# Clipped differences of the scan's sums on GpSimd, and 4 KB runs of the sums in DRAM

## The chip, the cores and the metric

The kernel runs on one core of one Trainium2 chip. The metric is the device time of one execution in microseconds. PE is TensorE, DVE is VectorE, ACT is ScalarE, POOL is GpSimd, SP is the engine that issues most transfers.

## The reference

Two layers of a streaming encoder for 256 prompt frames and 64 sample frames (320 columns in all). The first layer is a Mamba-2 mixer and a convolutional feed-forward network, the second a latent attention and another feed-forward network. The change lies in the mixer's scan. Its 32 heads are in four groups of eight, and time is cut into chunks. Within a chunk, with `acs` the running sum of `dt * a` of a head,

```python
seg = acs[:, :, :, None] - acs[:, :, None]
decay = jnp.exp(jnp.where(causal, seg, -jnp.inf))
wts = cb[..., None] * decay * dtc[:, :, None]
y_diag = jnp.einsum('bclsge,bcsgep->bclgep', wts, xc)
```

so each head needs a square of decays, the Exp of the difference of two sums, `acs` at the later frame minus `acs` at the earlier one. All differences that count are at most zero; where the later frame is the earlier one in the square, the entry is masked.

## The kernel before

Everything is transposed: features on the 128 partitions, frames in the free dimension. Weights are streamed once from DRAM by SP (`wr`, three buffers), split into a high and a low part by ACT (`wh`, L326) and DVE (`wl`, L328), four buffers of each, and used by PE in three matmuls each (L283, L284); a `block` is 24 such matmuls for one 128x320 result. PE has far more of this work than of any other.

The scan takes its frames in three chunks, two of 128 frames (prompt) and one of 64 (sample). `ssm_dt` forms `acs`, 96 rows (three chunks of 32 heads) by 128 frames; `ssm_dt2` (L837) writes it to DRAM as `acd` (L841) and transposes it on PE to `dtt` (L850), which so holds a column for each head and chunk. For each group and chunk `ssd_fetch` (L852) reads eight rows of `acd` back, to all 128 partitions at once: `dc`, 128 x 8 x n (L861). For the second and third chunk four rows each go to the two halves of `ea` (L866). Then, head by head (L874), ACT forms

`Relu(-dc + dtt column)`, the earlier sum less the later one, not below zero,

and `ssd_decay` (L878) takes Exp of its negative, one chunk at a time (through the helper `exp`, L673). DVE multiplies by the masked products of B and C (`bcs`, L909), and PE takes the products with `xa`, the inputs times `dt` (L932), and with the state (L940).

`ssd_steps` gives the order of one group's steps for its chunks: `pre` (L903 to L909), `xpose` (transposes L915 and the two DVE products L922 that give `xa` and `xw`), `diag` (L932; for the first chunk ACT empties the result to `yg`, L934; for the others L940 to L943), `states` (L949 and on). All of them take PSUM from a pool of two buffers (`px`).

Around it, `PLAN` (L28) is an order written out by hand: blocks of projections (`conv`, `z`) with `fetch`, `decay`, `scan`, `silu` and `gate` between. `work(n)` after each block emits n of the scan's late steps and, at a pace set by `fetch`, the heads' steps of L874. The Tile framework then orders each engine's instructions by a simulated timeline with costs of its own, within the dependences; `after` adds dependences without a wait, such as those of `exp` and `silu` (L667 to L675), which keep ACT's Exps and Silus together, since going from one to the other loads a table. Transfers of `acd` are held behind the current block (`issue`, L658).

POOL, before, does the small copies of the convolutions in this stage: the pads of `ext` (L636, L637), which ACT's L647 reads, and the rows saved for the state (L643, L644). Elsewhere it does some adds and, in the attention, weight splits.

Of the kernel before, what the change touches and what calls it, by code (L numbers as in the profile page):

```python
# [11 lines left out]
AF = mybir.ActivationFunctionType  # L12
ALU = mybir.AluOpType
# [3 lines left out]
P = 128  # L17
# [68 lines left out]
class Kern:  # L86
# [590 lines left out]
    def ssm(self):  # L677
        nc, a = self.nc, self.a
        self.silus, self.exps, self.burst = [], [], []
        self.yg, self.dc, self.ea = {}, {}, {}  # L680
        with ExitStack() as st:
            dr = st.enter_context(self.tc.tile_pool(name="acd", bufs=1, space=bass.MemoryType.DRAM))
            self.acd = self.t(dr, [96, P], "acd")
            ap = self.pool(st, "ssma")
            ah = self.t(ap, [P, 16, T], "ah", F32R)
            al = self.t(ap, [P, 16, T], "al", F32R)
            with ExitStack() as s2:
# [4 lines left out]
                with ExitStack() as s3:  # L692
# [3 lines left out]
                    for k in range(KD):  # L696
                        r = self.raw[k] = self.t(dp, [P, 512], "w0", bufs=KD)
# [76 lines left out]
            for half in range(2):  # L774
                w = [self.nextw(), self.nextw()]
                for n in range(4):
# [3 lines left out]
                    p = ps[3] if m == 7 else self.px()  # L780
                    for kb in range(12, 16):
# [4 lines left out]
                        q = slice((kb % 2 * 4 + n) * 128, (kb % 2 * 4 + n) * 128 + 128)  # L786
# [50 lines left out]
    def ssm_dt2(self, dt2, sp, dp):  # L837
        nc = self.nc
        dt, acs, w = dt2

        self.issue(nc.sync.dma_start(out=self.acd, in_=acs))  # L841
        self.cd = self.t(sp, [P, 3, 32], "cd")
        for p, n in ((slice(0, 64), 128), (slice(64, 96), 64)):
            self.exp(w[p, 0:n], acs[p, 0:n], scale=-1.0, bias=acs[p, n - 1:n])
        nc.vector.tensor_tensor(out=w, in0=w, in1=dt, op=ALU.mult)
        pd = self.px()
        for i, t_ in enumerate((dt, w, acs)):
            nc.tensor.transpose(pd[:, 96 * i:96 * i + 96], t_, self.ident[0:96, 0:96])
        self.dtt = self.t(sp, [P, 288], "dtt")
        nc.vector.tensor_copy(out=self.dtt, in_=pd[:, 0:288])  # L850

    def ssd_fetch(self, g, sp):  # L852

        nc = self.nc
        self.dc[g], self.ea[g] = {}, {}

        def load():
            for c, (_, n) in enumerate(CHUNKS):
                r0 = 32 * c + 8 * g
                dc = self.dc[g][c] = self.t(sp, [P, 8, n], f"dc{c}", bufs=DCB)  # L860
                self.issue(nc.sync.dma_start(out=dc, in_=self.acd[r0:r0 + 8, 0:n].partition_broadcast(P)))  # L861
                if c > 0:
                    ea = self.ea[g][c] = self.t(sp, [P, 4, n], f"ea{c}", bufs=DCB)
                    for odd in range(2):
                        r = r0 + 4 * odd
                        self.issue(nc.sync.dma_start(out=ea[64 * odd:64 * odd + 64], in_=self.acd[r:r + 4, 0:n].partition_broadcast(64)))  # L866

        def head(c, h):
            n = CHUNKS[c][1]
            dc = self.dc[g][c]  # L870
            q = 32 * c + 8 * g + h
            if c and h == 0:
                nc.vector.tensor_copy(out=self.cd[:, c, 8 * g:8 * g + 8].unsqueeze(2), in_=dc[:, :, n - 1:n])
            nc.scalar.activation(out=dc[:n, h, :], in_=dc[:n, h, :], func=AF.Relu, scale=-1.0, bias=self.dtt[:n, 192 + q:193 + q])  # L874

        return load, [lambda c=c, h=h: head(c, h) for c in range(3) for h in range(8)]

    def ssd_decay(self, g):  # L878

        cd = self.cd[:, 1:3, 8 * g:8 * g + 8]  # L880
        self.exp(cd, cd)
        for c, (_, n) in enumerate(CHUNKS):
            dc = self.dc[g][c]
            self.exp(dc[:n], dc[:n], scale=-1.0)
            if c > 0:
                self.exp(self.ea[g][c], self.ea[g][c])

# [624 lines left out]
```

## Time and profile before

| what | value |
|---|---|
| median of 3 runs | 1002.08 us (999.59 to 1002.16) |
| profiled execution, its own time | 1002.07 us |
| its span | 1000.3 us |
| granted clock, mean | 0.983 |
| PE busy | 960.9 us |
| DVE busy | 746.7 us |
| ACT busy | 620.4 us |
| POOL busy | 337.1 us |

The span runs from the first to the last recorded instruction; the time has some 1.8 us more around it. Busy times are of the whole span and hide stages in which another engine is the limit. In rows of the timeline the first number is the start in us, the second the duration in us of the x instructions on that row together, and the brackets give the engine's idle time before it and what ended that. In rows of groups the numbers after the bar are busy us and mean ns of one.

### The profile page before, as it was taken

Reading aid. Unit: us, or ns where it says so; the run is one execution under the profiler, and the core shown is the slowest. Engines: PE = TensorE matmul, PEld = TensorE weight load, DVE = VectorE, ACT = ScalarE, POOL = GpSimd, SP = SyncE. Lnnn points to the kernel's source line nnn. Section 1 sums busy time; section 2 is a strip of 40 time slices with the busy share of each in tenths; the row PEclk is TensorE's granted clock in tenths of the full one; section 3 lists DMA queues with packets and bytes.
Section 4 is the critical chain, followed back from the end, with each engine's and each line's share of the span. In section 5 each row is a group of like instructions: output and inputs, shape, how many; then the busy total and the mean of one; then the engine's idle time right before and its main releaser. Section 6 shows DMA issues by size and latency. Waiting matters only on the chain.

```text
span 1000.3 us, 18088 instructions
## 1 busy us (share of the span) xinstructions
PE 960.9 (96%) x6585; PEld 930.1 (93%) x6585; DVE 746.7 (75%) x1425; ACT 620.4 (62%) x1285; POOL 337.1 (34%) x597
## 2 busy tenths in 40 slices
PE   8897999999999999999999999999999999999995
PEld 7897999979989999999998899999999999999994
DVE  7865888887677998784538898886538999775433
ACT  6589797833555687664544677775544778664330
POOL 3921321100044775430005765530004766441001
PEclk9998999999999999999999999999999999999998
DMA  7374637353324444455641222233443455444531
GB/s 262 108 213 143 211 125 224 115 172 90 117 74 141 156 150 158 156 157 178 194 139 35 86 67 69 56 106 98 148 145 96 136 170 168 149 144 143 151 116 53
DMA packets 50905, 135.54 MB, mean 136 GB/s; under 512 B 11488, under 2 KB 15232, under 8 KB 50816
## 3 DMA queue, kind: packets, MB, share of 16 engines
q1 hardware_dynamic: 50528, 134.06, 42.6%
q8 instruction: 51, 0.84, 0.4%
q14 instruction: 38, 0.31, 0.1%
q10 hardware_dynamic: 288, 0.33, 0.1%
HBM read 130.25 MB, written 4.12 MB: 134 GB/s over the span
## 4 chain that ended last, share of the span: by engine, by line
PE 80%; DVE 9%; ACT 5%; POOL 3%; issue 2%; DMA 1%; SPq 0%; POOLq 0%; ACTq 0%; DVEq 0%
PE pm L283 46%; PE pm L284 23%; PE px L283 2%; PE px L932 1%; ACT wh L326 1%; PE px L949 1%; PE px L284 1%; POOL xacc L442 1%; PE pr L362 1%; PE px L940 1%; ACT dc L874 1%; DVE wl L328 1%; POOL xn L478 1%; DVE y L450 1%; DVE x L454 1%
## 5 line engine op out<-in xcount | busy, mean ns | idle before, releaser
L326 ACT ACTIVATE wh<-wr 128x1024 fp32r<-128x1024 f32 (+4 forms) x235 | 228.0, 973 | 160.0 <-PE pm L283 141.9
L328 DVE TENSOR_TENSOR wl<-wr,wh 128x1024 fp32r<-128x1024 f32 (+2 forms) x204 | 244.2, 1197 | 110.4 <-ACT wh L326 109.3
L283 PE MATMUL pm<-xnh,wh 128*128 128x320 f32 x784 | 243.4, 312 | 3.9 <-ACT xnh L329 3.2
L283 PE MATMUL pm<-xnl,wh 128*128 128x320 f32 x784 | 244.6, 312 | 0.3 <-DVE xnl L330 0.3
L284 PE MATMUL pm<-xnh,wl 128*128 128x320 f32 x784 | 243.4, 311 | 0.0
L283 PEld LDWEIGHTS pm<-xnh,wh 128*128 128x128 f32 x784 | 147.5, 189 | 6.5 <-ACT xnh L329 3.8
L284 PEld LDWEIGHTS pm<-xnh,wl 128*128 128x128 f32 x784 | 147.8, 189 | 1.7 <-issue 1.7
L283 PEld LDWEIGHTS pm<-xnl,wh 128*128 128x128 f32 x784 | 147.9, 189 | 1.3 <-issue 0.7
L283 PE MATMUL pm<-ah,wh 128*128 128x320 f32 x452 | 139.8, 311 | 1.7 <-ACT ah L329 1.7
L284 PE MATMUL pm<-ah,wl 128*128 128x320 f32 x452 | 140.6, 311 | 0.0
L283 PE MATMUL pm<-al,wh 128*128 128x320 f32 x452 | 140.4, 311 | 0.0
L649 DVE SCALAR_TENSOR_TENSOR cv<-ext,vec,cv 128x322 f32<-128x322 f32 x176 | 96.7, 563 | 5.4 <-ACT cv L647 3.0
L636 POOL MEMSET ext<- 128x2 f32 (+1 forms) x112 | 10.8, 98 | 245.9 <-DVE al L330 83.2
L643 POOL COPY fsave<-ext 128x2 f32<-128x2 f32 x88 | 72.5, 823 | 53.6 <-ACT ext L640 49.3
L283 PEld LDWEIGHTS pm<-ah,wh 128*128 128x128 f32 x452 | 84.7, 188 | 2.5 <-ACT ah L329 2.0
L283 PEld LDWEIGHTS pm<-al,wh 128*128 128x128 f32 x452 | 85.1, 188 | 1.0 <-issue 1.0
L284 PEld LDWEIGHTS pm<-ah,wl 128*128 128x128 f32 x452 | 85.1, 188 | 1.0 <-issue 1.0
L328 POOL TENSOR_TENSOR wl<-wr,wh 128x512 fp32r<-128x512 f32 (+2 forms) x31 | 43.6, 1424 | 102.3 <-ACT wh L326 100.9
L283 PE MATMUL pm<-xgl,wh 128*128 128x320 f32 x220 | 68.3, 314 | 1.0 <-DVE xgl L426 1.0
L284 PE MATMUL pm<-xgh,wl 128*128 128x320 f32 x220 | 68.2, 313 | 0.7 <-DVE wl L330 0.7
L283 PE MATMUL pm<-xgh,wh 128*128 128x320 f32 x220 | 62.5, 316 | 2.8 <-ACT wh L329 1.3
L647 ACT ACTIVATE cv<-ext,vec 128x322 f32<-128x322 f32 x88 | 57.1, 654 | 9.5 <-POOL ext L637 6.6
(395 smaller groups left out, 2132.4 us busy)
## 6 DMA issues: line engine op xcount, KB each, us to landing
wr<-w_up SPq DMA_DIRECT2D x76, 512.0 KB, 3.3
wr<-w_in SPq DMA_DIRECT2D x37, 512.0 KB, 3.7
wr<-w_dn SPq DMA_DIRECT2D x32, 512.0 KB, 3.6
wr<-w_out SPq DMA_DIRECT2D x16, 512.0 KB, 3.4
wr<-w_o SPq DMA_DIRECT2D x16, 512.0 KB, 3.4
wr<-w_up_k SPq DMA_DIRECT2D x16, 384.0 KB, 3.2
wr<-w_dn SPq DMA_DIRECT2D x16, 384.0 KB, 3.2
dc<-acd SPq DMA_DIRECT2D x8, 512.0 KB, 6.4
```

The lines of the kernel that those rows point to most:

```text
L283: for i in (mm(out, wh, xh, start=first, stop=False), mm(out, wh, xl, start=False, stop=False), mm(out, wl, xh, start=False, stop=last)):
L284: mm(out, wl, xh, start=False, stop=last)):
L326: self.high_ins = nc.scalar.activation(out=hdst, in_=src, func=AF.Copy).ins
L328: return lambda: e.tensor_tensor(out=ldst, in0=src, in1=hdst.bitcast(F32), op=ALU.subtract)
L362: i = self.nc.tensor.matmul(ps[:, o + b:o + b + 1], acc[:, l0:l0 + 128], self.ones[:, 0:1], start=True, stop=True)
L442: nc.gpsimd.tensor_tensor(out=acc, in0=acc, in1=s, op=ALU.add)
L450: tt(out=yk, in0=yk, in1=r, op=ALU.mult)
L454: e.tensor_tensor(out=xk, in0=xk, in1=yk, op=ALU.add)
L636: nc.gpsimd.memset(ext[:, 0:m], 0.0)
L643: nc.gpsimd.tensor_copy(out=rows_out[:, 0, :], in_=ext[:, TP:TP + m])
L647: nc.scalar.activation(out=c, in_=ext[:, 0:n], func=AF.Identity, scale=w(0), bias=b)
L649: nc.vector.scalar_tensor_tensor(out=c, in0=ext[:, i:i + n], scalar=w(i), in1=c, op0=ALU.mult, op1=ALU.add)
```

## The change

The Relu of a head on ACT becomes one operation on POOL: `dc` minus the column of `dtt`, then the minimum with zero. The result has the other sign, so Exp goes without its scale of -1. `acd` becomes two tiles in DRAM: 64 rows of 128 for the first two chunks, and 32 rows of 64 for the third, written by two transfers instead of one. All loads of `dc` and `ea` are written as one flat run: 4 KB for `dc` of the first two chunks, 2 KB of the third, and half of that for each half of `ea`.

```diff
@@ ssm @@
-            self.acd = self.t(dr, [96, P], "acd")
+            self.acd = self.t(dr, [64, P], "acd"), self.t(dr, [32, 64], "acd2")
@@ ssm_dt2 @@
-        self.issue(nc.sync.dma_start(out=self.acd, in_=acs))
+        self.issue(nc.sync.dma_start(out=self.acd[0], in_=acs[0:64]))
+        self.issue(nc.sync.dma_start(out=self.acd[1], in_=acs[64:96, 0:64]))
@@ ssd_fetch, load @@
-                r0 = 32 * c + 8 * g
+                r0 = 32 * (c % 2) + 8 * g
+                src = lambda a, b, p, c=c: self.acd[c // 2][a:b].rearrange("r l -> (r l)").partition_broadcast(p)
...
-                self.issue(nc.sync.dma_start(out=dc, in_=self.acd[r0:r0 + 8, 0:n].partition_broadcast(P)))
+                self.issue(nc.sync.dma_start(out=dc.rearrange("p h l -> p (h l)"), in_=src(r0, r0 + 8, P)))
...
-                    for odd in range(2):
-                        r = r0 + 4 * odd
-                        self.issue(nc.sync.dma_start(out=ea[64 * odd:64 * odd + 64], in_=self.acd[r:r + 4, 0:n].partition_broadcast(64)))
+                    for p, r in ((slice(0, 64), r0), (slice(64, 128), r0 + 4)):
+                        self.issue(nc.sync.dma_start(out=ea[p].rearrange("p h l -> p (h l)"), in_=src(r, r + 4, 64)))
@@ ssd_fetch, head @@
-            nc.scalar.activation(out=dc[:n, h, :], in_=dc[:n, h, :], func=AF.Relu, scale=-1.0, bias=self.dtt[:n, 192 + q:193 + q])
+            nc.gpsimd.tensor_scalar(dc[:n, h, :], dc[:n, h, :], self.dtt[:n, 192 + q:193 + q], 0.0, op0=ALU.subtract, op1=ALU.min)
@@ ssd_decay @@
-            self.exp(dc[:n], dc[:n], scale=-1.0)
+            self.exp(dc[:n], dc[:n])
```

## Prediction

> **What bounds the kernel now.** I read the table of busy time first, then the table by stage, then what PE waited for in the stage of the change, then the order of time on ACT and PE around the longest of these waits.
>
> ```profile
> span 1000.3 us, 18088 instructions
> PE 960.9 (96%) x6585; PEld 930.1 (93%) x6585; DVE 746.7 (75%) x1425; ACT 620.4 (62%) x1285; POOL 337.1 (34%) x597
> 54.00:84.00 30.00, 28.69 (x200) 27.00 (x198) 17.71 (x29) 27.27 (x68) 5.07 (x14) 1.00 0.85 247
> 84.00:92.00 8.00, 3.86 (x24) 3.16 (x25) 4.15 (x8) 7.99 (x23) 1.10 (x2) 0.63 0.00 1
> 92.00:132.00 40.00, 40.00 (x285) 37.51 (x284) 36.43 (x65) 33.95 (x77) 13.52 (x29) 0.99 0.58 191
> 132.00:182.00 50.00, 50.00 (x367) 46.51 (x362) 41.77 (x73) 42.10 (x89) 8.62 (x22) 1.00 0.57 172
> PE px L915 <- ACT yg L934: 3.7, 1, 3.7
> PE px L932 <- DVE xa L922: 1.5, 1, 1.5
> ```
>
> A stage row gives the stretch, its length, then PE, PEld, DVE, ACT and POOL busy, the granted clock, the DMA share and GB/s. PE bounds the kernel as a whole; the four groups of the scan, whose decays are loaded from 61 us on, lie between 54 and 245 us. From 92 to 182 us PE is busy without a gap, so an ACT that does less there can give nothing. Only between 84 and 92 us is PE half idle, while ACT is busy for 7.99 of 8 us: there ACT is the bound. The two waits say how: PE's transposes (L915) need a PSUM buffer that ACT's copy `yg` (L934) has yet to empty, and what follows needs `xa` from DVE. In order of time, ACT and then PE:
>
> ```profile
> 66.68 2.46 ACT L874 ACTIVATE dc<-dc,dtt 128x128 f32<-128x128 f32 x8 [2.32 <-DMA dc<-acd]
> 70.51 2.45 ACT L874 ACTIVATE dc<-dc,dtt 128x128 f32<-128x128 f32 x8
> 72.85 1.06 ACT L673 ACTIVATE dc<-dc 128x1024 f32<-128x1024 f32 x1
> 75.55 2.02 ACT L874 ACTIVATE dc<-dc,dtt 64x64 f32<-64x64 f32 x8
> 78.99 3.33 ACT L874 ACTIVATE dc<-dc,dtt 128x128 f32<-128x128 f32 x11
> 82.22 0.62 ACT L673 ACTIVATE dc<-dc 64x512 f32<-64x512 f32 x1
> 82.84 1.28 ACT L668 ACT_TABLE_LOAD   x1
> 84.14 1.27 ACT L668 ACTIVATE sz<-sz 128x1280 f32<-128x1280 f32 x1
> 86.04 0.57 ACT L934 ACTIVATE yg<-px 128x512 f32<-128x512 f32 x1
> 89.52 1.05 ACT L326 ACTIVATE wh<-wr 128x1024 fp32r<-128x1024 f32 x1
> 82.67 0.30 PE L284 MATMUL pm<-xnh,wl 128*128 128x320 f32 x1
> 86.67 1.11 PE L915 MATMUL px<-con,xs 128*128 128x128 f32 x4 [3.70 <-ACT yg L934]
> 89.25 1.98 PE L932 MATMUL px<-dc,xa 128*64 128x128 f32 x16 [1.47 <-DVE xa L922]
> 91.16 1.99 PE L940 MATMUL px<-ct,hp 128*128 128x128 f32 x8
> 92.89 0.41 PE L283 MATMUL pm<-xnh,wh 128*128 128x320 f32 x1
> 131.23 1.02 PE px L932 x16
> 137.46 0.44 PE px L915 x4
> 144.11 0.89 PE px L940 x8
> ```
>
> The last three rows, from the chain of waits, are the same PE work in a dense stretch. From 82.97 (82.67 and 0.30) to 92.89 us PE does in 9.92 us what it does elsewhere in 0.44 + 1.02 + 0.89 = 2.35 us. Of the difference, 3.70 us are the wait for `yg` and 1.47 the wait for `xa`. The rest is the granted clock, 0.63 in this stage: L915 takes 1.11 and not 0.44 (0.67 lost), L932 1.91 to the start of L940 and not 1.02 (0.89 lost), L940 1.73 to the next matmul and not 0.89 (0.84 lost). [...]
>
> **The change part by part.** *Removed from ACT:* 96 Relus.
>
> ```profile
> L874 ACT ACTIVATE dc<-dc,dtt x96: 332/388/407, 66.7 to 173.1; 128x128 f32<-128x128 f32 x64, 64x64 f32<-64x64 f32 x32
> ```
>
> In a row eight of them take 2.46 us (128 wide) or 2.02 us (64 wide), so ACT loses 2.46 + 2.45 + 2.02 = 6.93 us a group, 27.7 in all. What counts is what goes ahead of `yg` at 86.04: 2.46 + 2.45 + 2.02 + 3.33 = 10.26 us of Relus, and the 2.32 us in which ACT waited for the load.
>
> *Added to GpSimd:* the same 96 as subtract-and-min, 24 a group. The trace has no such instruction; the nearest rows on POOL are these, and two that show who waits for whom:
>
> ```profile
> L1126 POOL CAST cql<-cql x3: 236/236/1302, 553.8 to 554.7; 128x64 fp32r<-128x64 f32 x3
> L1199 POOL TENSOR_TENSOR qs<-q,qs 32x256 fp32r<-32x256 f32 x16 | 11.8, 738 | 1.0
> L1199 POOL TENSOR_TENSOR qs<-q,qs 32x64 fp32r<-32x64 f32 x16 | 6.0, 378 | 1.0
> L637 POOL COPY ext<-vec 128x3 f32<-128x3 f32 x24 | 16.9, 713 | 0.2 <-issue 0.2
> 110.39 0.18 POOL L643 COPY ssave<-ext 128x3 f32<-128x3 f32 x1
> 105.98 4.47 POOL L637 COPY ext<-vec 128x3 f32<-128x3 f32 x1
> 106.00:110.40 4.40, 4.40 (x45) 4.14 (x44) 4.40 (x8) 3.18 (x7) 4.40 (x3) 1.00 0.49 173
> 66.70:80.00 13.30, 13.30 (x96) 12.45 (x96) 7.01 (x14) 13.30 (x41) 1.91 (x8) 1.00 1.02 258
> 556.83 1.59 DVE L1132 TENSOR_TENSOR qacc<-qacc,xsq 128x320 f32<-128x320 f32 x1 [0.46 <-DVE qacc L1132]
> ```
>
> Low end: a copy of 3 columns takes 0.18 us and a cast of 64 takes 0.236, so 0.9 ns a column, 0.295 us for 128 and 0.236 for 64: 16 x 0.295 + 8 x 0.236 = 6.6 us a group. From two-input operations: 378 ns at 64 columns and 738 at 256 give 498 at 128, so 16 x 0.498 + 8 x 0.378 = 11.0 us. High end: the 3-column copies take 0.713 us on average, 0.53 above the undisturbed one, and one took 4.47 while DVE was busy for 4.40 of 4.40 us. With that wait on each, 6.6 + 24 x 0.53 = 19.3 us, or 23.7 on the dearer base. I take 12 us for the first group: its DVE has room. Between 66.7 and 80 us DVE is busy for 7.01 us, of which the `xa` step (1.29 us, row below) reads PSUM; if POOL waits out the other 5.7, the group takes 6.6 + 5.7 = 12.3 us. [...]
>
> *On the path.* POOL starts when ACT did, at 66.68. From the last Exp of the group to `yg` ACT needs 86.04 - 82.22 = 3.82 us (Exp, table load, three Silus). PE is ready for the buffer at 82.97, so the wait vanishes if POOL is done by 79.15, that is, if 24 operations take 12.5 us; at 15.5 us (0.65 us each) `yg` is where it was. With 12 us `yg` starts at 82.5: the 3.70 us go and with them the cause of the low clock, 0.67 + 0.89 + 0.84 = 2.40 us. What is late next is `xa`: its 1.47 us stay, as the DVE step lies between transposes and products in any case. Gain 3.70 + 2.40 = 6.1 us. It is kept only if the weights come earlier too: the split at 89.52 stands behind all the Relus above and moves forward with them, and DVE, idle before 87.8 us, has room.
>
> ```profile
> 87.82 1.29 DVE L922 TENSOR_TENSOR xa<-px,dtt 128x512 f32<-128x512 f32 x2 [7.47 <-PE px L915]
> 124.69 1.22 DVE L328 TENSOR_TENSOR wl<-wr,wh 128x1024 fp32r<-128x1024 f32 x1
> 129.18 0.31 PE L284 MATMUL pm<-xnh,wl 128*128 128x320 f32 x1
> ```
>
> *The other groups.* PE has no gap there, so I cost 72 operations at nothing; their cover is the lead of the weights. Counting splits against blocks of 24 matmuls, it is mostly 5 to 12 us and shortest at the last two rows, 129.18 - 125.91 = 3.27 us. Behind the new operations on POOL's queue stand the pads of the convolutions (L636, L637); ACT's L647 waits for those, and the weight splits for ACT.
>
> *The layout.* The loads of 128-column chunks are in one run already: a row of `acd` has 128 numbers. Only the 64-column chunk changes, from 256 B to 2 KB (`ea` 1 KB).
>
> ```profile
> DMA packets 2639, 3.69 MB, mean 275 GB/s; under 512 B 1710, under 2 KB 1710, under 8 KB 2638
> 55.07 0.43 SPq L841 DMA_DIRECT2D acd<-acs  x1
> 56.14 5.22 SPq L191 DMA_DIRECT2D wr<-w_in  x3
> ```
>
> The first row is the stretch from 60 to 73.4 us: 1710 small packets and 928 between 2 and 8 KB bear this out. The third chunk comes earlier, but POOL is at the first two until then: nothing on the path. The store becomes two issues on SP; the second (0.43 us) fits before 56.14, since the first ends at 55.50. Dropping the minus sign in Exp costs nothing.
>
> The sum: the profiled execution took 1002.07 us, its span 1000.3 and 1.8 around it, beside a median of 1002.08, so the two can be taken as one. 1002.07 - 6.1 = 996.0 us.
>
> **The rivals.** *GpSimd is starved.* If each operation waits for DVE as the 3-column copies do, 24 take 21.6 us at 0.9 us each, the group is done at 88.3, `yg` starts at 92.1 and PE waits 6.1 us longer: about 1008 us. It decides above 0.65 us an operation. For it speaks the 4.47 us row, against it that DVE is busy only 17.71 of 30 us there.
>
> [...]
>
> *The wait survives.* The order on each engine is set by a planner from its own costs; with operations moved, `yg` may be put behind the Silus and further splits again, so that ACT is as late as before: about 1002 us, no change.
>
> **How the numbers follow.** No change means within 0.3%, 3 us. The wait goes: 0.54. DVE gives back: 0.12. The wait survives: 0.10. Starved: 0.24. Faster: 0.54 and a quarter of the second case, 0.57; slower: nearly all of the last, 0.23; the remaining 0.20 is no change. The low bound takes off the 1.47 us of `xa` too and a further 1 us elsewhere: 993.5. Up to 1005, halfway into the starved case, lie 0.54 + 0.12 + 0.10 and a fifth of the last, 0.81. The likeliest case alone spans 993.5 to 998.
>
> **What would show it.** Right: L874 on POOL at 0.3 to 0.5 us; the last Exp of the first group before 79.5 us; no wait of L915 for `yg` over 1 us; the clock at 1.0 from 84 to 92 us; ACT down by some 28 us. Wrong: L874 at 0.65 us or more, L673 or L647 waiting for POOL, DVE's L328 and L649 longer on average, or PE waiting for `wl` after 92 us.

## The result and the profile after

The changed kernel takes 1012.86 us (median of 4 runs, 1011.58 to 1014.38), the kernel before on the same chip 1002.12 us: ratio 1.0114, 95% interval 1.0093 to 1.0134. The forecast was 996.0 us and a range to 1005, so it is wrong in sign and the time lies outside the range. One execution of all that are reported below, of the kernel with group 1's Relus later, took 2638.67 us where no other took over 1016.97; it is left out of that kernel's median. The profiled execution took 1011.58 us, 1009.8 of it the span. In the changed kernel lines up to L841 have the numbers of before and those from the heads' step on are one higher: L875 is the clipped difference, L935 `yg`, L916 the transposes.

The table of busy time, and then the table by stage with the columns explained in the prediction:

```profile
span 1009.8 us, 18107 instructions
PE 962.3 (95%) x6585; PEld 932.0 (92%) x6585; DVE 749.3 (74%) x1425; ACT 597.2 (59%) x1189; POOL 419.1 (42%) x693
```

```profile
84.00:92.00 8.00, 8.00 (x67) 7.64 (x66) 4.90 (x7) 5.05 (x5) 8.00 (x10) 1.00 0.73 237
92.00:132.00 40.00, 32.04 (x209) 28.55 (x209) 31.97 (x59) 25.50 (x49) 37.95 (x56) 0.91 0.46 150
132.00:182.00 50.00, 49.37 (x352) 46.16 (x353) 43.34 (x75) 34.19 (x63) 32.39 (x50) 1.00 0.47 150
182.00:222.00 40.00, 35.65 (x257) 32.88 (x257) 26.49 (x46) 23.50 (x34) 11.21 (x23) 0.96 0.39 124
```

The stall of before is gone: from 84 to 92 us PE is busy for all of 8 us at full clock (before 3.86 us at 0.63). The stages that were dense before have holes instead: 32.04 of 40 us from 92 to 132 (before 40.00), 35.65 of 40 from 182 to 222, for which the kernel before had

```profile
182.00:222.00 40.00, 39.45 (x291) 35.72 (x289) 34.55 (x65) 23.61 (x36) 0.00 (x0) 1.00 0.48 161
```

The new operations, by shape (busy us, mean ns) and then over all of them (min/median/max ns), are far dearer than assumed:

```profile
L875 POOL TENSOR_SCALAR dc<-dc,dtt 128x128 f32<-128x128 f32 x64 | 65.5, 1039 | 6.7 <-DMA dc<-acd 6.7
L875 POOL TENSOR_SCALAR dc<-dc,dtt 64x64 f32<-64x64 f32 x32 | 21.2, 679 | 0.0
```

```profile
L875 POOL TENSOR_SCALAR dc<-dc,dtt x96: 490/708/3700, 67.0 to 192.7; 128x128 f32<-128x128 f32 x64, 64x64 f32<-64x64 f32 x32
```

And ACT now waits for POOL's small copies, which it never did here before. The waits from 60 to 245 us (total, times, longest), then rows in order of time:

```profile
ACT xs L647 <- POOL ext L637: 16.7, 5, 7.8
ACT ext L640 <- POOL ssave L644: 9.0, 2, 4.9
PE px L933 <- DVE xa L923: 7.1, 3, 4.4
PE pm L283 <- ACT ext L640: 5.3, 2, 4.0
```

```profile
67.04 13.35 POOL L875 TENSOR_SCALAR dc<-dc,dtt 128x128 f32<-128x128 f32 x16 [1.00 <-DMA dc<-acd]
83.00 0.58 ACT L935 ACTIVATE yg<-px 128x512 f32<-128x512 f32 x1
89.03 0.63 ACT L673 ACTIVATE dc<-dc 64x512 f32<-64x512 f32 x1 [2.48 <-DMA wr<-w_in]
```

And some hundred us later:

```profile
183.44 7.88 POOL L875 TENSOR_SCALAR dc<-dc,dtt 128x128 f32<-128x128 f32 x13
191.31 0.18 POOL L637 COPY ext<-vec 128x3 f32<-128x3 f32 x1
191.53 0.66 ACT L647 ACTIVATE xs<-ext,vec 128x323 f32<-128x323 f32 x1 [7.83 <-POOL ext L637]
197.41 1.25 PE L933 MATMUL px<-dc,xa 128*64 128x128 f32 x16 [4.35 <-DVE xa L923]
```

Two things are to be seen. `yg` starts at 83.00 us, but the group's last Exp only at 89.03 (before 82.22): `yg` is early because ACT issues it ahead of that Exp, not because POOL is fast. And at 183 us thirteen operations of the last group run on POOL, behind them the pad of a convolution; ACT waits 7.83 us for that pad, and at the end of that chain PE waits for `xa`.

### The profile page after: what moved, and what is told of

The parts are those of the page before. It is cut to its first block, busy times and chain, and to the rows that moved or that the text cites. A ratio compares the mean times of both kernels' runs of the same rounds, so it can differ in the third digit from the quotient of the medians.

```text
span 1009.8 us, 18107 instructions
## 1 busy us (share of the span) xinstructions
PE 962.3 (95%) x6585; PEld 932.0 (92%) x6585; DVE 749.3 (74%) x1425; ACT 597.2 (59%) x1189; POOL 419.1 (42%) x693
## 2 busy tenths in 40 slices
DMA packets 45802, 135.54 MB, mean 134 GB/s; under 512 B 5392, under 2 KB 9616, under 8 KB 45712
## 4 chain that ended last, share of the span: by engine, by line
PE 68%; DVE 13%; POOL 10%; issue 4%; ACT 4%; DMA 1%; SPq 0%; POOLq 0%; ACTq 0%; DVEq 0%
PE pm L283 40%; PE pm L284 20%; POOL dc L875 7%; PE px L283 2%; DVE wl L328 2%; ACT wh L326 1%; PE px L284 1%; PE pr L362 1%; POOL xacc L442 1%; DVE xs L649 1%; POOL xn L478 1%; DVE cv L649 1%; DVE y L450 1%; DVE x L454 1%; PE px L941 1%
## 5 line engine op out<-in xcount | busy, mean ns | idle before, releaser
L328 DVE TENSOR_TENSOR wl<-wr,wh 128x1024 fp32r<-128x1024 f32 (+2 forms) x204 | 243.9, 1196 | 116.3 <-ACT wh L326 115.5
L284 PE MATMUL pm<-xnh,wl 128*128 128x320 f32 x784 | 244.2, 312 | 0.0
L284 PEld LDWEIGHTS pm<-xnh,wl 128*128 128x128 f32 x784 | 148.2, 189 | 0.9 <-issue 0.9
L284 PE MATMUL pm<-ah,wl 128*128 128x320 f32 x452 | 140.4, 311 | 0.0
L649 DVE SCALAR_TENSOR_TENSOR cv<-ext,vec,cv 128x322 f32<-128x322 f32 x176 | 97.7, 570 | 5.5 <-ACT cv L647 3.2
L875 POOL TENSOR_SCALAR dc<-dc,dtt 128x128 f32<-128x128 f32 (+1 forms) x96 | 86.6, 919 | 6.7 <-DMA dc<-acd 6.7
L328 POOL TENSOR_TENSOR wl<-wr,wh 128x512 fp32r<-128x512 f32 (+2 forms) x31 | 43.7, 1425 | 102.3 <-ACT wh L326 100.9
L284 PEld LDWEIGHTS pm<-ah,wl 128*128 128x128 f32 x452 | 84.9, 188 | 1.1 <-issue 1.0
L284 PE MATMUL pm<-xgh,wl 128*128 128x320 f32 x220 | 68.6, 315 | 1.0 <-DVE wl L330 0.7
```

The costliest lines, as they stand in the source:

```text
L284: mm(out, wl, xh, start=False, stop=last)):
L328: return lambda: e.tensor_tensor(out=ldst, in0=src, in1=hdst.bitcast(F32), op=ALU.subtract)
L649: nc.vector.scalar_tensor_tensor(out=c, in0=ext[:, i:i + n], scalar=w(i), in1=c, op0=ALU.mult, op1=ALU.add)
L875: nc.gpsimd.tensor_scalar(dc[:n, h, :], dc[:n, h, :], self.dtt[:n, 192 + q:193 + q], 0.0, op0=ALU.subtract, op1=ALU.min)
```

## The experiments

The k-th matmul of L284 that reads `xnh` and `wl` (the mixer's projections) marks the same amount of work in every kernel, so its start says how far a kernel is ahead of before (negative) or behind. All times are worked out from the rows of PE in order of time, in us. The 89th is in the first block after the stall, the 265th near the end of these projections; the scan goes on to 245 us. Behind the scan the table would mislead: two kernels with before's order that are level with it up to the 265th (layout alone, pads on DVE) are 2.4 and 2.2 us ahead of the profiled execution of before from 331 us on, though their medians are the same as its own.

| kernel | median | ratio (interval) | 89th | 145th | 177th | 233rd | 265th |
|---|---|---|---|---|---|---|---|
| before, starts at | 1002 | 1 | 93.28 | 122.84 | 141.41 | 173.09 | 193.81 |
| after | 1012.86 | 1.0114 (1.0093-1.0134) | -9.0 | +4.9 | +7.2 | +6.1 | +11.0 |
| layout alone, planner's order | 1013.13 | 1.0104 (1.0079-1.013) | -0.4 | +0.1 | -0.4 | +0.5 | -1.6 |
| POOL operations, old layout, planner's order | 1008.73 | 1.0072 (1.0055-1.0088) | -6.8 | +8.3 | +10.9 | +11.1 | +10.1 |
| POOL in group 0 only, planner's order | 1006.18 | 1.0045 (1.0031-1.0058) | -7.7 | -7.1 | -8.6 | -7.1 | -8.6 |
| POOL in groups 1 to 3 only, planner's order | 1013.61 | 1.0118 (1.0096-1.014) | -6.5 | -3.5 | -4.4 | +4.0 | +7.0 |
| layout alone, before's order | 1001.21 | 1.0 (0.9987-1.0013) | -0.2 | +0.4 | +0.4 | +0.4 | +0.4 |
| whole change, before's order | 1016.30 | 1.0145 (1.0124-1.0166) | +1.9 | +2.0 | +4.6 | +5.6 | +14.3 |
| the same, pads on DVE | 1004.56 | 1.0024 (1.001-1.0037) | +2.8 | +3.2 | +3.2 | +3.4 | +3.8 |
| group 0 on DVE, before's order | 995.35 | 0.9937 (0.9912-0.9961) | -5.0 | -4.9 | -4.9 | -4.9 | -4.9 |
| after's own order, pads on DVE | 1003.43 | 1.0009 (0.9996-1.0023) | -8.0 | +3.6 | +5.1 | +4.1 | +3.0 |
| before, pads on DVE | 1002.13 | 1.0005 (0.9993-1.0017) | +0.4 | +0.7 | +0.7 | +0.7 | +0.7 |
| before, group 1's Relus later | 997.68 | 0.996 (0.9946-0.9974) | -2.7 | -2.5 | -2.5 | -2.6 | -2.6 |
| group 0 on DVE, Relus later, transposes early | 995.05 | 0.9937 (0.9919-0.9956) | -7.3 | -7.1 | -7.1 | -7.2 | -7.2 |

### The change in parts, ordered by the planner

Layout alone, Relus left on ACT (the edit is against the changed kernel):

```diff
-            nc.gpsimd.tensor_scalar(dc[:n, h, :], dc[:n, h, :], self.dtt[:n, 192 + q:193 + q], 0.0, op0=ALU.subtract, op1=ALU.min)
+            nc.scalar.activation(out=dc[:n, h, :], in_=dc[:n, h, :], func=AF.Relu, scale=-1.0, bias=self.dtt[:n, 192 + q:193 + q])
...
-            self.exp(dc[:n], dc[:n])
+            self.exp(dc[:n], dc[:n], scale=-1.0)
```

> Only the DRAM layout of the change (two stores, flat loads); the Relus stay on ACT. Theory (the new operations on POOL are the whole of the change's effect): 1002 us, within 3 us of before. Rival (the loads' shape or the second store costs or gains): outside 999 to 1005 us, with the first Exp of the third chunk moved by 2 us or more.

Measured 1013.13 us, a miss. It runs level with before up to the 265th matmul (-1.6) and ends 11.7 us behind; the place is the last group's scan and the gate behind it, where few blocks are left. That stage in this kernel, and then before:

```profile
222.00:245.00 23.00, 17.53 (x92) 13.20 (x93) 14.90 (x33) 3.84 (x8) 0.00 (x0) 0.70 0.07 24
```

```profile
222.00:245.00 23.00, 21.26 (x148) 18.71 (x148) 18.28 (x31) 8.45 (x14) 0.23 (x2) 0.93 0.19 58
```

PE is busy for 17.53 us at a clock of 0.70 and not for 21.26 at 0.93. What differs there is the order in which the engines are given their instructions; that the order alone makes the difference is tested below. The other three were:

```diff
 POOL operations, old layout: the line above on POOL, acd and its loads as before
 group 0 only:       if g == 0: nc.gpsimd.tensor_scalar(...)   else: Relu on ACT
 groups 1 to 3 only: if g > 0:  nc.gpsimd.tensor_scalar(...)   else: Relu on ACT
```

> Only the operations on POOL, in the old layout. Theory: as the changed kernel, 1010 to 1015 us. Rival (layout matters): under 1008 or over 1017 us.

> New layout; GpSimd does the clipped differences of group 0 only, ACT those of groups 1 to 3. Theory (group 0 gains some 9 us by block 14, and the loss comes from groups 1 to 3, whose 24 operations of 0.71 and 0.49 us stand before the convolutions' pads and saves on POOL's queue): 992 to 998 us, PE's wait of L915 for yg gone, ACT's waits for POOL under 3 us. [...]

> New layout; ACT does group 0, GpSimd groups 1 to 3. Theory: group 0 keeps its wait and the loss of groups 1 to 3 stays, 1014 to 1023 us, or less where ACT's head start in group 1 comes later; ACT's L640 and L647 wait for POOL by 15 us or more. [...]

Measured 1008.73, 1006.18 and 1013.61 us; none lies in a range that was expected of it. The signs on POOL's queue did hold: from 60 to 245 us ACT waits for no POOL copy with group 0 only, and for 19.1 us with groups 1 to 3 only. But the parts do not add up. With groups 1 to 3 only, the first group's Relus are all still on ACT, and yet most of the stall at 83 us is gone (-6.5):

```profile
80.52 0.65 ACT L673 ACTIVATE dc<-dc 64x512 f32<-64x512 f32 x1
84.37 1.99 ACT L326 ACTIVATE wh<-wr 128x1024 fp32r<-128x1024 f32 x2
86.26 0.57 ACT L938 ACTIVATE yg<-px 128x512 f32<-128x512 f32 x1
89.62 0.60 PE L919 MATMUL px<-con,xs 128*128 128x128 f32 x4
```

`yg` is no earlier than before (86.04). But the eleven Relus of the second group that stood ahead of it (3.33 us) have left ACT, and the planner put two weight splits ahead of it, so PE works on blocks in the meantime and does not wait at the transposes. So each of these kernels differs from before by its edit and by another order of some 10,000 instructions, and none of them isolates a part. With group 0 only, 7 to 9 us are gained and held up to the 265th matmul, and are then lost in the tail as in the run of the layout.

### The same parts in before's order

For the next runs each engine's order of instructions was taken from the kernel before, written out and enforced by dependences without a wait (`add_manual_dep(i, last[engine], NOSYNC)` for each instruction in turn); a clipped difference stands where its Relu stood. Lines move by this, a little differently in each kernel: the clipped difference is at L900 to L904, the pads' copy at L644 or L645, ACT's copy into `ext` at L647 or L648, the convolution's first step on ACT at L654 or L655, Exp at L699 or L700, the transposes at L941 to L945, `yg` at L960 to L964, the blocks at L289 and L290, the split `wl` at L334.

> The new layout of the sums alone, Relus on ACT, and each engine's instructions in the order that the kernel before has, written out by hand, so that the planner cannot move anything. Theory (the 11 us that the layout cost alone were the planner's other order behind 212 us): 999 to 1005 us, PE from 222 to 245 us about as busy as before. Rival (the layout itself costs, by its second store or by the flat loads): 1008 us or more.

1001.21 us, every block of the table within 0.4 us of before: the layout by itself costs and gives nothing, and the 11 us above were the order.

> The whole change with each engine in the order of the kernel before; each POOL operation stands where the Relu stood in the order of all instructions. Theory 1 (POOL's price, 0.71 us and not 0.5, and the convolutions' pads and saves that stand behind the new operations on POOL's queue cost time by themselves): 1005 to 1020 us, with ACT's L647 and L640 waiting for POOL and PE not dense between 92 and 182 us. Theory 2 (all of the loss is the planner's order): 994 to 1000 us, as forecast.

1016.30 us. Theory 1: the loss does not need the planner. Three places make it up, +1.9 at the stall, 3.6 us between the 145th and the 233rd matmul, and 8.7 behind that. The stages of the first and of the longest one:

```profile
84.00:92.00 8.00, 2.25 (x16) 1.88 (x18) 2.65 (x6) 7.98 (x16) 8.00 (x16) 0.57 0.00 0
182.00:222.00 40.00, 33.37 (x240) 30.65 (x240) 28.25 (x49) 23.54 (x36) 10.53 (x20) 0.91 0.36 117
```

The longest one in order of time:

```profile
175.53 16.17 POOL L903 TENSOR_SCALAR dc<-dc,dtt 128x128 f32<-128x128 f32 x16
191.69 0.18 POOL L644 COPY ext<-vec 128x3 f32<-128x3 f32 x1
191.91 0.66 ACT L654 ACTIVATE xs<-ext,vec 128x323 f32<-128x323 f32 x1 [10.53 <-POOL ext L644]
196.26 0.58 ACT L981 ACTIVATE hp<-px 128x512 f32<-128x512 f32 x1
196.90 0.42 PE L932 MATMUL px<-con,bt 128*64 128x128 f32 x1 [6.63 <-ACT hp L981]
```

A copy of three columns that takes 0.18 us waits behind 16 operations; ACT stands still for 10.53 us for it, `hp` comes late behind that on ACT, and PE waits 6.63 us for the PSUM buffer that `hp` empties.

Then the same kernel with the mixer's pads and saved rows on DVE:

```diff
-        nc.gpsimd.memset(ext[:, 0:m], 0.0)
-        nc.gpsimd.tensor_copy(out=ext[:, q:q + m], in_=pads)
+        e = nc.vector if k == 4 else nc.gpsimd
+        e.memset(ext[:, 0:m], 0.0)
+        e.tensor_copy(out=ext[:, q:q + m], in_=pads)
...
-        nc.gpsimd.tensor_copy(out=rows_out[:, 0, :], in_=ext[:, TP:TP + m])
+        e.tensor_copy(out=rows_out[:, 0, :], in_=ext[:, TP:TP + m])
...
```

> As the whole change in before's order, but the mixer's pads (L636, L637) and saved rows (L643, L644) are copied by DVE, so nothing that ACT waits for stands behind the new operations on POOL. Queue theory: at least 6 us less than the same kernel with the pads on POOL, no wait of L647 or L640 for POOL. [...]

1004.56 us, 11.7 us less: the queue theory. What remains arises at the stall (+3.2) and hardly grows (+3.8 at the 265th matmul): from 92 to 222 us PE is as dense as before, with POOL's 72 other operations beside it.

```profile
92.00:132.00 40.00, 40.00 (x276) 37.94 (x275) 37.48 (x89) 27.94 (x53) 26.49 (x27) 0.94 0.53 174
132.00:182.00 50.00, 50.00 (x362) 46.47 (x362) 43.63 (x97) 33.52 (x60) 25.70 (x27) 1.00 0.53 172
182.00:222.00 40.00, 39.93 (x294) 36.29 (x293) 36.08 (x64) 24.78 (x36) 9.93 (x10) 1.00 0.51 164
```

```profile
66.85 32.02 POOL L904 TENSOR_SCALAR dc<-dc,dtt 128x128 f32<-128x128 f32 x40 [21.70 <-DMA dc<-acd]
84.62 0.63 ACT L700 ACTIVATE dc<-dc 64x512 f32<-64x512 f32 x1 [3.05 <-POOL dc L904]
88.45 0.58 ACT L964 ACTIVATE yg<-px 128x512 f32<-128x512 f32 x1
89.08 1.12 PE L945 MATMUL px<-con,xs 128*128 128x128 f32 x4 [5.09 <-ACT yg L964]
```

The first group's 24 operations take from 66.85 to about 84.6 us, 17.8 us; the Exp waits 3.05 us for them, `yg` is 2.4 us later than before, and PE's wait grows from 3.70 to 5.09 us.

The control, before's kernel with the same pads on DVE:

> Control: the kernel before in its own order, Relus on ACT, only the pads and saved rows on DVE instead of POOL. If the 12 us that this edit gave back in the whole change are the queue behind the clipped differences, it gives nothing here: 1000 to 1003 us. If pads on DVE are quicker in themselves (0.06 to 0.17 us against 0.71 on average), it gives several us here too: 996 us or less.

1002.13 us, ratio 1.0005: the pads are not better on DVE as such; they are only better away from the new operations.

### Where the changed kernel itself lost

The edit of the pads once more, now on the changed kernel with its own order held fixed.

> The changed kernel in its own order of instructions (not before's), with one edit: the mixer's pads and saved rows (L637, L638, L644, L645 of the changed kernel) are copied by DVE, so that nothing stands behind the clipped differences on POOL. In the changed kernel the block at 95 us is 9.0 us early and all is lost between 92 and 222 us, by 14 us. Queue theory: the 9 us are kept up to 212 us, no wait of ACT for a pad; at most 5 to 10 us are lost behind 212 us by the planner's order there: 996 to 1003 us. [...]

1003.43 us, 9.4 us less than the changed kernel; just above the expected range, though the expectation was wrong on the place. By the table the pads cost little in the middle and most behind 177 us (+7.2 to +11.0 with them, +5.1 to +3.0 without). But the loss between the 89th and the 145th matmul, 13.9 us in the changed kernel, stays at 11.6 with the pads away. In before's order the same POOL operations lose 0.4 us in that stretch, so they do not cost it by themselves: it needs the order that the planner made. Whether that order would lose it without them was not tried; by the table the two kernels in a planner's order with all 96 operations on POOL lose 13.9 and 15.1 us there, those with a part of them or none 0.5 to 3.0 us. One of its places, in this kernel:

```profile
116.00:120.00 4.00, 1.54 (x13) 1.30 (x11) 4.00 (x9) 3.99 (x6) 4.00 (x3) 1.00 0.53 161
```

```profile
115.75 1.28 ACT L700 ACT_TABLE_LOAD   x1
117.17 1.99 ACT L700 ACTIVATE dc<-dc 128x1024 f32<-128x1024 f32 x2
120.41 0.47 ACT L648 ACTIVATE ext<-pm 128x256 f32<-128x256 f32 x2
120.93 0.42 PE L289 MATMUL pm<-xnh,wh 128*128 128x320 f32 x1 [3.38 <-ACT ext L648]
```

A block's PSUM stands full while ACT goes through the table load and six Exps of the next group, and PE waits 3.38 us for it. Why the planner put them so was not tried.

### Two ways to have the gain

The first group's clipped differences on DVE, the rest as before:

```diff
+            if g == 0:
+                nc.vector.tensor_scalar(dc[:n, h, :], dc[:n, h, :], self.dtt[:n, 192 + q:193 + q], 0.0, op0=ALU.subtract, op1=ALU.min)
+            else:
                 nc.scalar.activation(out=dc[:n, h, :], ..., func=AF.Relu, ...)
...
+            self.exp(dc[:n], dc[:n], scale=1.0 if g == 0 else -1.0)
```

> Before's order and before's layout; only the first group's 24 clipped differences are moved, and to DVE, which is busy for 17.7 of 30 us there; the others stay Relus on ACT. Theory (the stall at 83 to 93 us is ACT's, and only group 0 gains by taking work off ACT): the wait of L915 for yg goes, the end of the scan stays as before, 993 to 997 us. Rival (the gain is lost behind, as it was in every kernel so far): 1000 to 1004 us.

995.35 us, ratio 0.9937 (0.9912 to 0.9961): faster than both kernels.

```profile
66.37 1.66 DVE L901 TENSOR_SCALAR dc<-dc,dtt 128x128 f32<-128x128 f32 x8 [0.41 <-DMA dc<-acd]
78.14 0.62 ACT L699 ACTIVATE dc<-dc 64x512 f32<-64x512 f32 x1
81.97 0.57 ACT L963 ACTIVATE yg<-px 128x512 f32<-128x512 f32 x1
85.00 1.10 PE L961 MATMUL px<-dc,xa 128*64 128x128 f32 x16 [1.47 <-DVE xa L951]
88.29 0.42 PE L290 MATMUL pm<-xnh,wl 128*128 128x320 f32 x1 [0.75 <-DVE wl L334]
```

Here is what the prediction described: the last Exp at 78.14, `yg` at 81.97, the 1.47 us for `xa` left over, and 4.9 us gained that are kept at every later block.

The second way leaves all Relus on ACT and moves only group 1's 24 out of the stall. ACT's order, with the line numbers and times of the kernel before:

```diff
-  hp, 11 Relus, Exp, Silus, yg, xs, 1 Relu, L647, 4 Relus, bcs, 2 Relus, split, ext, 6 Relus, split, ...
+  hp, Exp, Silus, yg, xs, L647, bcs, split, ext, split, ..., L647 (97.3 us), 6 Relus, split, 6 Relus, split, 8 Relus, split, 4 Relus
```

> The kernel before in its order, but for one move on ACT: the second group's 24 Relus, which run between 79.0 and 92.4 us among the work that PE waits for, are issued behind L647 at 97.3 us and behind the three weight splits that follow (6, 6, 8 and 4 of them), where ACT is idle for 6.0 us; their Exps start at 109.7 us. Nothing goes to another engine. Theory (the stall at 83 to 93 us is the order on ACT, not ACT's load): yg comes 3.3 us earlier, the clock holds, 995 to 998 us. Rival (ACT's load moves with it, to the Exps at 110 us): 1000 to 1004 us.

997.68 us, ratio 0.996 (0.9946 to 0.9974). `yg` came 1.5 us earlier, not 3.3, as ACT waited 4.1 us for a load of `dc` and not 2.32; the wait of PE fell from 3.70 to 1.69 us and the clock held (1.00 from 84 to 92 us):

```profile
85.21 0.66 PE L941 MATMUL px<-con,xs 128*128 128x128 f32 x4 [1.69 <-ACT yg L960]
```

Both together, and on PE the four transposes moved up (line numbers of the kernel before):

```diff
-  bc (L903, L904), 11 matmuls of the block, transposes L915, diag L932
+  bc (L903, L904), transposes L915, 11 matmuls of the block, diag L932
```

> The first group's clipped differences on DVE, as in the run that gave 995.35 us, the second group's Relus later on ACT, and on PE the four transposes L915 for the second chunk some 12 matmuls earlier, so that DVE forms xa while PE still has blocks to work on. Theory (what is left of the stall there are the 1.47 us for xa and 0.75 us for wl): 2 us less again, 992 to 994.5 us. Rival (the Relus that come later delay the next group): 995 us or more.

995.05 us, expected 992 to 994.5: a miss in the total. In the trace the stall is down to one wait of 0.74 us for `wl`, the blocks are 7.1 us ahead of before, 2.3 us more than in the run with DVE alone; the medians, 995.05 and 995.35, do not tell the two kernels apart.

## Why the prediction was wrong

*"What bounds the kernel now": right.* PE's stall at 83 to 93 us was ACT's, from 92 to 182 us an ACT that does less gives nothing, and taking the first group's 6.9 us off ACT is worth about what was worked out (6.1 us forecast; 4.9 at the blocks and 6.6 in the median with DVE doing them).

*"Added to GpSimd", the price: the first term that was mis-sized.* I took 12 us for a group. In the changed kernel's trace the median of the 128-wide operations is 0.712 us and of the 64-wide ones 0.493: 16 x 0.712 + 8 x 0.493 = 15.3 us, all but the 15.5 at which, by the prediction's own account, the gain is nothing. Measured in before's order it is 17.8. The account itself held: 84.62 + 3.82 = 88.44 us for `yg`, measured 88.45. The mistake was to bound a subtract-and-min with a scalar of each partition by copies of 3 and 64 columns; per column it costs (0.712 - 0.493) / 64 = 3.4 ns, not 0.9.

*"The other groups. I cost 72 operations at nothing": the step that failed most.* The operations as such cost next to nothing there (+3.2 at the 145th matmul, +3.8 at the 265th, with the pads elsewhere). The prediction named the pads as queued behind them and the ACT line that waits, and then put no price on it. Its price is 11.7 us in before's order and 9.4 in the changed kernel's, most of the loss. What should have been multiplied out: the runs of 13 and 16 operations ahead of a pad took 7.88 and 16.17 us, and the cover named was 3.27 to 12.

*"On the path": right in outcome, wrong in cause.* The wait for `yg` did go and the clock held (1.00 from 84 to 92 us), but because the planner issued `yg` ahead of the last Exp, which was luck: in before's order the wait grew. The marks that I had set for it disagreed: L875 is at 0.708 at the median of all and the last Exp at 89.03, where I wanted 0.3 to 0.5 and 79.5. That the wait was the cause of the low clock, the 2.40 us of the sum, was an estimate: no run shows what lowers the clock. What the runs have from 84 to 92 us is a clock of 0.63 in the kernel before with its wait of 3.70 us for `yg`, 0.57 in the whole change in before's order with one of 5.55 us, and 1.00 with one of 1.69 us (group 1's Relus later) and in the changed kernel, where PE does not wait for `yg`; the four transposes take 1.11, 1.12, 0.66 and 0.63 us in these.

*"The layout": right*, 1001.21 us; packets under 512 B fall from 11488 to 5392 and no one was waiting for them.

*The rivals.* "GpSimd is starved" came nearest: 0.9 us an operation on average in the changed kernel, as it supposed. But its place was wrong; `yg` is not where that time went. "DVE gives back", the case of 0.12, is seen only to a small part: DVE's L328 takes as long as before (1228 ns against 1226) and L649, with two inputs, 17 ns longer on average, while POOL's 128-wide operations have a mean of 1.039 us against a median of 0.712. The rows of before and then of the changed kernel:

```profile
L328 DVE TENSOR_TENSOR wl<-wr,wh 128x1024 fp32r<-128x1024 f32 x162 | 198.5, 1226 | 84.0 <-ACT wh L326 83.3
L649 DVE SCALAR_TENSOR_TENSOR xs<-ext,vec,xs 128x323 f32<-128x323 f32 x48 | 25.5, 549 | 0.2
```

```profile
L328 DVE TENSOR_TENSOR wl<-wr,wh 128x1024 fp32r<-128x1024 f32 x162 | 198.8, 1228 | 92.0 <-ACT wh L326 91.7
L649 DVE SCALAR_TENSOR_TENSOR xs<-ext,vec,xs 128x323 f32<-128x323 f32 x48 | 26.5, 566 | 18.9 <-ACT xs L647 18.7
```

On POOL's side the changed kernel's trace shows more. Of its 64 operations of 128 columns, the 23 without a DVE operation on two SBUF inputs beside them took 0.703 to 0.716 us, and the 23 that took over 0.8 us all had one; the longest, 3.70 us, ended 0.51 us after the last of four DVE operations that ran one behind the other. On DVE's side the rows show a loss of 2 and 17 ns. "The wait survives through the planner's order" had the right agent and the wrong sign and place: the order gave 9.0 us at the stall, and in it 11.6 us went again by the 145th matmul even with the pads away.

What stays open is what makes the middle loss of the changed kernel, 11.6 us with the pads away; it was shown only that before's order with the same operations does not have it.

## What to carry to other kernels

An operation moved to an idle engine takes its place in that engine's queue: price what stands behind it by the length of the whole run (here 16 x 1.0 us against pads of 0.18 us), and move such small feeders to another engine, or ahead, before counting the engine as free. Where a planner orders the instructions, every edit also draws another order, here worth 11.7 us for an edit that by itself costs nothing; hold the order fixed before putting a time down to a part. And take the price of an operation from one with the same operands: here the copies and casts gave 0.9 ns a column, and the operation with a scalar of each partition took 3.4.

## What the runs showed of the hardware

A subtract-and-min with a column of scalars took 0.71 us on POOL for 128 columns, 0.49 for 64 (medians); on DVE 1.66 / 8 = 0.21 us and as a Relu on ACT 2.46 / 8 = 0.31, both for 128. Over the changed kernel's scan the POOL operation on 128 columns took up to 3.70 us and 1.04 on average, and never over 0.716 us where no DVE operation on two SBUF inputs ran beside it; DVE's rows L328 and L649 lengthened by 2 and 17 ns on average over the whole kernel. The flat runs of 2 and 4 KB moved no block by more than 0.4 us here.
